# A chunked recurrence with its odd heads stored in the other order: paired products, state and output in one product, right-looking inverses

## The chip, the core and the metric

The kernel runs on one core of one Trainium2 chip. A core has a tensor engine (PE, with its weight loads shown apart as PEld), a vector engine (DVE), a scalar engine (ACT), GpSimd (POOL) and a sync engine (SP), which here issues nearly all DMAs. Each engine runs its instructions in order. The metric is device time in microseconds (us), lower is better.

## The reference

One gated block over S = 2048 tokens of width 1024. Its input projection feeds two branches: an RWKV-7 recurrence with 8 heads of 64 (the part that changes), and an attention over 256 selected keys per query. The recurrence is, for each head, with a 64x64 state:

```python
def rwkv7_scan(r, w, k, v, a_vec, b_vec):
    def step(state, inp):
        r_t, w_t, k_t, v_t, a_t, b_t = inp
        sa = jnp.einsum('bhvk,bhk->bhv', state, a_t)
        state = (state * w_t[:, :, None, :] + sa[..., None] * b_t[:, :, None, :]
                 + v_t[..., None] * k_t[:, :, None, :])
        y_t = jnp.einsum('bhvk,bhk->bhv', state, r_t)
        return state, y_t
...
    _, y = lax.scan(step, s0, xs)

def rwkv7_branch(...):
    ...
    y = rwkv7_scan(r_h, w_h, k_h, v_h, -kk, kk * a_h)
    yn = ((y - mu) * lax.rsqrt(var + GN_EPS)).reshape(B, S, RWKV_WIDTH) * lnx_g + lnx_b
```

The outputs of both branches are gated, projected, summed and normed.

## The kernel before

The tokens lie in 4 blocks `tb` of 512. The recurrence runs over 32 chunks of 64 tokens, 8 to a block, all in float32. Three functions do it.

`rwkv_pass(tb)` makes, for each pair of heads `p`, the decayed factors `ar` and `bk` and their products of 128x128 per head and chunk (L698, tile `pg`), masks them and stores them in DRAM (`gmd`), with `ard`, `bkd`, `vtd` beside them. The even head of a pair sits in rows 0 to 63 of the tensor engine (hh = 0), the odd one in rows 64 to 127 (hh = 1).

`rwkv_inv(tb)` loads the 128 triangular blocks of 32x32 of a token block, one to a partition (16 loads, L725), and inverts them by 31 steps of a multiplication (L733) and a sum (L735) on DVE, then stores them (`tid`, `ttd`, L738 to L740).

`rwkv_chain(tb)` is the recurrence proper. For each chunk it issues 7 loads, then, for all 8 heads: two steps that make the off-diagonal block of the inverse (L770 and L775, 32x32, tile `zu`), the state times the chunk's `ar` (L781, four products of 128x128, a pair of heads at a time, the state `H` held as blocks on a diagonal), `gmc` times v (L784), copied to `xx` (L787, ACT), the inverse times `xx` (L790), copied to `uv` (L791, DVE), the state update (L794, four products of 128x128 into `hp`, added to the decayed state by L798 on POOL and L799 on DVE), and the output (L801, into the same bank `pp` as L781 and L784, copied to `y` by L806). `H` is what one chunk hands to the next. Every second chunk is normed, every fourth goes through `chain_out` (transposes, L837). Its PSUM pool (`pc`) holds one bank each for `zu`, `pp` and `hp`.

Beside it run the projection GEMM (`gemm_half`, L251, three passes of 256 tokens), the keys and values of attention (`heads`, L868 and L878, tile `p`), and later the first branch's output projection (`branch_a`, L1092, tile `br`) and attention (from L925 on).

No order is written by hand: a scheduler puts the instructions of each engine in order by priority. `self.band(n)` sets the priority of what is emitted after it, a lower number first, and among equals what is emitted first:

```python
        self.band(50000)
        self.rwkv_chain(0)
        self.band(60000)
        self.cut = 2
        self.gemm_half((2, 3), ("rkv",))
        self.band(55000)
        self.rwkv_pass(2)
        self.rwkv_inv(2)
        self.band(55000)
        self.rwkv_chain(1)
        self.rwkv_pass(3)
        ...
        self.rwkv_inv(3)
        self.rwkv_chain(2)
        self.rwkv_chain(3)
        self.band(70000)
        self.gemm_half((2, 3), ("q",))
```

## Time and profile before

| what | value |
|---|---|
| time, median of 3 runs | 2611.75 us (2610.64 to 2611.93) |
| span of the profiled execution | 2605.7 us |
| PE busy | 2449.8 us, 94% of the span |
| DVE, ACT, POOL busy | 1750.5 (67%), 1229.8 (47%), 868.2 us (33%) |
| matmul instructions | 16776 |
| DMA packets, mean rate | 423499, 160 GB/s |

The span runs from the first to the last instruction; of the profiled execution only the span is recorded, and the median of the runs lies 6.05 us above it. Busy is the time in which an engine had an instruction in flight. Matmuls overlap in its pipeline, so in a full queue what a product costs is the distance from its start to the next one's start, and not its own length. A float32 product on PE runs as two passes and is shown as two instructions: eight products are an entry "x16".

### The profile page before, as it was taken

To read this page: it belongs to the slowest core of one execution; us is meant where nothing else is said; L and a number is where in the kernel's file an instruction comes from. 1 tells how busy PE (TensorE), PEld (TensorE's weight loads), DVE (VectorE), ACT (ScalarE), POOL (GpSimd) and SP (SyncE) were. 2 spreads that over 40 slices of the span, in tenths; PEclk is the share of its full clock that TensorE was granted. 3 is DMA by queue.
4 is the path that set the end of the run, shared out by engine and by line. 5 is a ranking of instruction groups with operands and counts; after the bars stand their busy time and mean duration, and the time that the engine had idled before them with its cause. 6 is when DMAs were issued, how large, how long until landed. Compare 5 with 4: busy or idle time off the path is not lost. (4 is left out here: it accounts for less than half of the span.)

```text
span 2605.7 us, 45357 instructions
## 1 busy us (share of the span) xinstructions
PE 2449.8 (94%) x16776; PEld 2153.8 (83%) x16776; DVE 1750.5 (67%) x3509; ACT 1229.8 (47%) x2136; POOL 868.2 (33%) x707
## 2 busy tenths in 40 slices
PE   4899999989899999899999999999989999999998
PEld 3687777868677899689898888988978999988887
DVE  6615888798988355774956947533468888877443
ACT  4315636446344423324334233343367888865332
POOL 2311131241323333223233322131155545645342
PEclk9999999999999999899999999999999999999999
DMA  7754222522233756568677669977763334145442
GB/s 245 271 149 127 77 85 73 131 77 88 84 103 102 243 162 202 147 192 234 179 219 204 187 189 284 293 233 189 239 199 116 91 88 118 45 152 195 147 150 77
DMA packets 423499, 415.69 MB, mean 160 GB/s; under 512 B 80010, under 2 KB 339890, under 8 KB 418404
## 3 DMA queue, kind: packets, MB, share of 16 engines
q1 hardware_dynamic: 422692, 404.33, 51.7%
q0 software_dynamic: 576, 8.39, 0.8%
q8 instruction: 132, 2.16, 0.4%
q14 instruction: 99, 0.81, 0.1%
HBM read 254.04 MB, written 160.15 MB: 159 GB/s over the span
## 5 line engine op out<-in xcount | busy, mean ns | idle before, releaser
L251 PE MATMUL g<-hh,whi 128*128 128x256 f32 (+1 forms) x2176 | 726.9, 334 | 14.8 <-DVE eo L265 4.5
L251 PE MATMUL g<-hl,whi 128*128 128x256 f32 (+1 forms) x2176 | 722.5, 332 | 3.9 <-POOL hl L169 2.4
L251 PE MATMUL g<-hh,wlo 128*128 128x256 f32 (+1 forms) x2176 | 721.0, 331 | 1.2 <-POOL wlo L237 1.2
L251 PEld LDWEIGHTS g<-hh,whi 128*128 128x128 f32 x2176 | 421.4, 194 | 63.8 <-issue 5.7
L251 PEld LDWEIGHTS g<-hl,whi 128*128 128x128 f32 x2176 | 421.0, 193 | 47.6 <-issue 3.9
L251 PEld LDWEIGHTS g<-hh,wlo 128*128 128x128 f32 x2176 | 420.7, 193 | 42.7 <-issue 3.9
L237 POOL TENSOR_TENSOR wlo<-wraw,whi 128x1024 fp32r<-128x1024 f32 (+1 forms) x89 | 216.9, 2437 | 629.4 <-ACT whi L236 583.0
L421 ACT ACTIVATE re<-ixs 128x512 f32<-128x512 f32 (+3 forms) x304 | 158.9, 548 | 176.1 <-DVE sc L427 109.8
L427 DVE SCALAR_TENSOR_TENSOR sc<-re,wi,sc 128x512 f32<-128x512 f32 (+3 forms) x266 | 222.6, 842 | 21.7 <-ACT re L421 6.5
L236 ACT CAST whi<-wraw 128x1024 fp32r<-128x1024 f32 (+1 forms) x89 | 92.8, 1042 | 175.1 <-PE g L251 131.0
L957 PE MATMUL pt<-ident,lt 128*128 128x128 f32 x1088 | 168.2, 276 | 6.4 <-ACT tp L963 3.5
L947 ACT ACTIVATE lt<-lt,nm 128x128 f32<-128x128 f32 (+15 forms) x128 | 154.7, 1211 | 14.2 <-DVE nm L946 14.1
L943 DVE CUSTOM_DVE_ANT_0 lt<-lg,mask 128x512 f32<-128x512 f32 (+3 forms) x256 | 147.4, 590 | 15.9 <-PE lg L941 7.5
L974 PE MATMUL yv<-ph,vp 128*128 128x256 f32 (+1 forms) x576 | 151.5, 285 | 6.7 <-ACT yl L978 4.7
L968 DVE TENSOR_TENSOR pl<-pt,ph 128x512 fp32r<-128x512 f32 (+1 forms) x216 | 139.1, 657 | 25.7 <-ACT ph L967 24.6
L974 PE MATMUL yv<-pl,vp 128*128 128x256 f32 x576 | 152.4, 300 | 2.0 <-POOL pl L965 2.0
L418 PE MATMUL ixs<-kim,st 128*128 128x512 f32 (+3 forms) x304 | 117.3, 387 | 28.7 <-ACT re L421 24.8
L940 PE MATMUL lg<-m,sq 128*128 128x256 f32 (+3 forms) x384 | 137.2, 366 | 5.0 <-DVE cm L943 4.1
L957 PEld LDWEIGHTS pt<-ident,lt 128*128 128x128 f32 x1088 | 125.9, 141 | 15.6 <-ACT tp L963 4.5
L941 PE MATMUL lg<-m,sq 128*128 128x256 f32 (+3 forms) x384 | 127.4, 337 | 0.0
L733 DVE TENSOR_TENSOR prd<-tm,ln 128x1 f32<-128x1 f32 (+30 forms) x124 | 113.3, 914 | 20.5 <-DMA pk<-pj 14.6
L967 ACT CAST ph<-pt 128x512 fp32r<-128x512 f32 (+1 forms) x216 | 115.9, 565 | 19.7 <-PE pt L957 13.7
(347 smaller groups left out, 5391.4 us busy)
## 6 DMA issues: line engine op xcount, KB each, us to landing
wraw<-in_w_in_dram SPq DMA_DIRECT2D x88, 512.0 KB
gg<-eo SPq DMA_DIRECT2D x64, 256.0 KB
gmd<-gt SPq DMA_DIRECT2D x64, 256.0 KB
gmc<-gmd SPq DMA_DIRECT2D x32, 512.0 KB
g<-gg SPq DMA_DIRECT2D x64, 256.0 KB
m<-ks SPq DMA_DIRECT2D x32, 512.0 KB
pj<-eo SPq DMA_DIRECT2D x52, 256.0 KB
x<-in_ada_w_dram SPq DMA_DIRECT2D x24, 512.0 KB
```

The lines of the kernel that those rows point to most:

```text
L237: nc.gpsimd.tensor_tensor(lo[:, :, :n], raw[:, :, :n], hi[:, :, :n].bitcast(FT), op=OP.subtract)
L251: T.matmul(p[:, s], a[:, k], b[:, k, s], start=n == 0, stop=n == 3 * KD - 1)
L418: T.matmul(p[:, :kn], st[:, h], M[0][:, k0:k0 + kn], start=True, stop=False)
L421: A.activation(r[:, :kn], p[:, :kn], AF.Relu)
L427: V.scalar_tensor_tensor(o, r[:, :kn], wi, o, op0=OP.mult, op1=OP.add)
L940: T.matmul(p[:, :kn], sq[:, qb * 128:(qb + 1) * 128], m1[:, k0:k1_], start=True, stop=False)
L941: T.matmul(p[:, :kn], sq[:, qb * 128:(qb + 1) * 128], m2[:, k0:k1_], start=False, stop=True)
L943: V.tensor_tensor_reduce(lt[:, k0:k1_], p[:, :kn], mk, 1.0, -3.0e38, OP.add, OP.max, cm[:, i:i + 1])
L947: ex = A.activation(lt[:, :n], lt[:, :n], AF.Exp, bias=nm, accum_out=lsum[:, qb, h:h + 1])
L957: T.transpose(p[:, o:o + 128], L[i][:, kt * 128:(kt + 1) * 128], self.ident)
L968: V.tensor_tensor(pl[:, :n], p[:, :n], ph[:, :n].bitcast(FT), op=OP.subtract)
L974: T.matmul(yv[:, qs], vp[:, kt, :], b[:, o:o + nn], start=kt == 0 and i == 0, stop=kt == last and i == 1, skip_group_check=True)
```

## The change

The odd heads get the other order of rows and columns: what lies in rows 0 to 63 for an even head lies in rows 64 to 127 for an odd one, and so do the halves of its output. A pair of products can then stand in different rows and different columns of the tensor engine. With it:

- `rwkv_pass` emits the products of both heads of a pair alternately, into two banks (L709).
- `rwkv_inv` is right-looking: step s takes column s from all later rows (L747 multiply, L749 add), (31-s)(s+1) elements a step.
- `rwkv_chain` is rewritten. `chunk_loads` fetches the next chunk's operands with 19 DMAs (7 before) into two buffers `cb0` and `cb1` made by hand, with `ttc0` and `ttc1`. `chunk_off` (L800, L807) and `chunk_v` (L820, L823) prepare the next chunk. Per chunk there follow the state times `ar` (L850: 8 products, each 64 rows and 128 columns of weights, 64 columns moving), the inverse (L857), and one product for state update and output together (L866: 8 products, 128 rows and 128 columns of weights, 64 columns moving). The state `H` is stored without the zero blocks. The copies are spread over ACT and DVE, and the output is added on DVE (L881).
- Norms and `chain_out` of a block wait in a list and are emitted a chunk later. The PSUM pool of the chain has 4 banks held for all time (`X0` to `X3`), and that of `heads` 2 instead of 3.
- Bands: the chains get 45000 and 47000 instead of 50000 and 55000, and chain 0 is emitted after the GEMM `rkv` of the second half.

```diff
@@ rwkv_pass
+                pts = [pg((128, 4, 128)) for hh in range(2)]
+                for j in range(4):
+                    for hh in range(2):
+                        r_ = slice(hh * 64, hh * 64 + 64)
+                        T.matmul(pts[hh][:, j], bk[r_, c0 + j, :], ar[r_, c0 + j, :], start=True, stop=True)
@@ rwkv_inv
-        for t in range(1, 32):
-            v = prd[:, :t * t].rearrange("p (j s) -> p j s", j=t)
-            V.tensor_tensor(v, tm[:, 0:t, 0:t].rearrange("p s j -> p j s"),
-                            ln[:, 0:t, t][:, None, :].to_broadcast([128, t, t]), op=OP.mult)
-            V.tensor_reduce(tm[:, t, 0:t], v, axis=AX, op=OP.add)
+        for s in range(31):
+            r, n = 31 - s, s + 1
+            v = prd[:, :r * n].rearrange("p (t j) -> p t j", t=r)
+            V.tensor_tensor(v, ln[:, s, n:][:, :, None].to_broadcast([128, r, n]),
+                            tm[:, s, 0:n][:, None, :].to_broadcast([128, r, n]), op=OP.mult)
+            V.tensor_tensor(tm[:, n:, 0:n], tm[:, n:, 0:n], v, op=OP.add)
@@ chunk_loads, chunk_off, chunk_v (new)
+        for a, b in ((E, O), (O, E)):
+            DMA.dma_start(cb[a, :, 2], src[b, :, 0, 0])
+            DMA.dma_start(cb[a, :, 1], src[b, :, 0, 1])
+        DMA.dma_start(cb[:, :, 4:6], src[:, :, 1])
...
+                T.matmul(zp[o + 32:o + 64, p], cb[64 - o:96 - o, p, 2 + 2 * e, 32:64], t1c[64 - o:96 - o, p],
+                         start=True, stop=True)
@@ rwkv_chain
+            if not last:
+                nxt = R["v"] = self.chunk_loads(tb + (c == 7), (c + 1) % 8)
...
             for p in range(4):
-                T.matmul(pp[:, p * 128:(p + 1) * 128], arc[:, p, :], H0[:, p, :], start=p == 0, stop=False,
-                         skip_group_check=True)
+                for e in range(2):
+                    r_ = halves[e]
+                    T.matmul(pp[e][:, p], arc[r_, p], H0[r_, p], start=False, stop=p == 3, skip_group_check=True)
...
+            up = X[2][:, 0:256].rearrange("q (p v) -> q p v", p=4)
             for p in range(4):
-                T.matmul(hp[:, p], bkc[:, p * 128:(p + 1) * 128], uv[:, p * 128:(p + 1) * 128], start=True, stop=True)
+                for e, r_ in enumerate(halves):
+                    T.matmul(up[halves[1 - e], p], ttc[r_, p], xx[r_, p], start=True, stop=True)
...
+            mg = X[2].rearrange("q (p e v) -> q p e v", p=4, e=2)
+            for e in range(2):
+                for p in range(4):
+                    T.matmul(mg[:, p, e], cb[:, p, 5 * e:5 * e + 2].rearrange("q g t -> q (g t)"), uv[:, p, e],
+                             start=True, stop=True)
...
+            if not last:
+                self.chunk_off(nxt)
+                self.chunk_v(nxt)
@@ the order
-        self.band(50000)
-        self.rwkv_chain(0)
...
-        self.band(55000)
+        self.band(45000)
+        self.rwkv_chain(0)
+        self.band(57000)
+        self.rwkv_pass(3)
+        self.rwkv_inv(3)
+        self.R["pctx"].close()
+        self.band(47000)
         self.rwkv_chain(1)
```

How the order moves, at three places. On PE before, the last product of the projections (L251) stands ahead of the state update of chunk 28 (L794); then the output of that chunk (L801) and `branch_a` (L1092):

```order
L790 MATMUL zu<-xx,ttc 64x64 x8
L251 MATMUL g<-hl,whi 128x256
L251 MATMUL g<-hh,wlo 128x256
L251 MATMUL g<-hh,whi 128x256
L251 MATMUL g<-hl,whi 128x256
L251 MATMUL g<-hh,wlo 128x256
L794 MATMUL hp<-uv,bkc 128x128 x4
L801 MATMUL pp<-uv,gmc 64x64 x8
L1092 MATMUL br<-uh_19482,w_pah 128x256
L1092 MATMUL br<-ul_19483,w_pah 128x256
L1092 MATMUL br<-uh_19482,w_pah 128x256
```

Here 28 of 32 chunks lie beside the projections. In the change the last L251 stands behind the merged product of chunk 24 (L866), and only the products of `heads` (L952, L962) are left beside chunks 25 to 32:

```order
L866 MATMUL X_9188<-uv,cb_9182 128x64 x8
L251 MATMUL g<-hl,whi 128x256
L251 MATMUL g<-hh,wlo 128x256
L251 MATMUL g<-hh,whi 128x256
L251 MATMUL g<-hl,whi 128x256
L251 MATMUL g<-hh,wlo 128x256
L850 MATMUL X_9186<-H_9174,arc 128x64 x4
L850 MATMUL X_9187<-H_9174,arc 128x64 x4
L952 MATMUL p<-lat_16844,w_ukh 128x512 x2
L952 MATMUL p<-lat_16846,w_ukh 128x512 x2
L952 MATMUL p<-lat_16844,w_ukl 128x512 x2
```

So four more chunks stand behind the end of the projections. The next place is the end of the chain on PE. Before, one of the last chunks stands like this, with products of `branch_a` (L1092) between its steps:

```order
L1092 MATMUL br<-ul_19767,w_pah 128x256
L1092 MATMUL br<-uh_19766,w_pal 128x256
L781 MATMUL pp<-H_9176,arc 128x128 x2
L775 MATMUL zu<-ttc,t1c 32x32 x8
L781 MATMUL pp<-H_9176,arc 128x128 x2
L784 MATMUL pp<-uv,gmc 64x64 x8
L1092 MATMUL br<-uh_19766,w_pah 128x256
L1092 MATMUL br<-ul_19767,w_pah 128x256
L1092 MATMUL br<-uh_19766,w_pal 128x256
L1092 MATMUL br<-uh_19766,w_pah 128x256
```

Other work fills PE between the steps. In the change the last two chunks and the start of `branch_a` (there L1176) read so:

```order
L857 MATMUL X_9188<-xx,ttc_9178 64x64 x8
L866 MATMUL X_9188<-uv,cb_9176 128x64 x8
L850 MATMUL X_9186<-H_9180,arc 128x64 x4
L850 MATMUL X_9187<-H_9180,arc 128x64 x4
L919 MATMUL X_9188<-ident,y 128x128 x4
L857 MATMUL X_9188<-xx,ttc_9184 64x64 x8
L866 MATMUL X_9188<-uv,cb_9182 128x64 x8
L1176 MATMUL br<-uh_19830,w_pah 128x256 x2
L1176 MATMUL br<-ul_19831,w_pah 128x256
```

No L1176 stands ahead of the last L866 any more, and a chunk's steps follow each other with nothing between them but transposes (L919). A little earlier two chunks mesh: L807 and the first half of L820 of one chunk stand ahead of the merged product of the chunk before it:

```order
L850 MATMUL X_9186<-H_9180,arc 128x64 x4
L850 MATMUL X_9187<-H_9180,arc 128x64 x4
L800 MATMUL X_9189<-t1c,cb_9176 32x32 x7
L857 MATMUL X_9188<-xx,ttc_9184 64x64
L820 MATMUL X_9186<-uv,cb_9176 128x64
L823 MATMUL X_9186<-uv,cb_9176 64x64 x3
L857 MATMUL X_9188<-xx,ttc_9184 64x64 x7
L807 MATMUL X_9189<-ttc_9178,z 32x32 x8
L820 MATMUL X_9187<-uv,cb_9176 128x64
L823 MATMUL X_9187<-uv,cb_9176 64x64 x3
L866 MATMUL X_9188<-uv,cb_9182 128x64 x8
```

The third place is the SP queue late in the chain, one chunk's loads. Before, 7 of them, with other transfers between:

```order
L1118 DMA gg_81<-g 128x2x256
L764 DMA ttc<-ttd_9205 32x8x32
L765 DMA ttc<-ttd_9205 32x8x32
L1095 DMA g<-gg_82 128x2x256
L1118 DMA gg_81<-g 128x2x256
L1095 DMA g<-gg_82 128x2x256
L757 DMA bkc<-bkd_9189 128x512
L755 DMA gmc<-gmd_9181 128x1024
L759 DMA uv<-vtd_9193 64x512
L1118 DMA gg_81<-g 128x2x256
L766 DMA t1c<-tid_9201 32x8x32
```

Between a chunk's loads stand those of `branch_a`. In the change 19 to a chunk; the buffer `cb` named here is read by the merged product two chunks back:

```order
L765 DMA cb_9182<-gmd_9193 64x4x64 x2
L766 DMA cb_9182<-gmd_9193 128x4x128
L769 DMA uv<-vtd_9205 64x4x64
L770 DMA uv<-vtd_9205 64x4x64
L787 DMA cb_9182<-bkd_9201 64x4x64
L788 DMA cb_9182<-bkd_9201 64x4x64
L789 DMA cb_9182<-bkd_9201 128x4x64
L773 DMA arc<-ard_9197 64x512
L774 DMA arc<-ard_9197 64x4x64
L775 DMA arc<-ard_9197 64x4x64
L785 DMA ttc_9178<-ttd_9217 32x4x32 x3
L765 DMA cb_9176<-gmd_9193 64x4x64 x2
```

Whatever stands behind a load that waits for its buffer waits too.

## Rows read from the trace of the kernel before

**Rows 1.** Windows: stretch, length, busy per engine, TensorE clock, DMA share, GB/s.
```profile
1165.60:1748.00 582.40, 576.31 (x5506) 525.93 (x5505) 366.11 (x568) 215.11 (x364) 181.97 (x170) 0.99 0.75 224
1748.00:1829.60 81.60, 72.75 (x703) 67.76 (x702) 32.14 (x51) 27.36 (x45) 16.41 (x16) 0.90 0.74 209
1829.60:1890.80 61.20, 59.25 (x492) 58.77 (x491) 26.44 (x44) 20.25 (x32) 7.76 (x6) 0.97 0.70 225
1890.80:2605.70 714.90, 681.46 (x4592) 619.71 (x4592) 500.79 (x1373) 470.17 (x863) 349.50 (x346) 0.98 0.41 125
```

**Rows 2.** Timeline, PE, 1773 us: start, length, what ran.
```profile
1773.51 1.05 PE L794 MATMUL hp<-uv,bkc 128*128 128x128 f32 x8
1774.49 1.15 PE L801 MATMUL pp<-uv,gmc 128*64 128x64 f32 x16
1775.57 0.69 PE L770 MATMUL zu<-t1c,gmc 32*32 32x32 f32 x16
1776.18 0.39 PE L1092 MATMUL br<-uh,w_pal 128*128 128x256 f32 x1
```

**Rows 3.** Timeline, PE, 1779 us, the same block of tokens.
```profile
1779.95 0.94 PE L781 MATMUL pp<-H,arc 128*128 128x128 f32 x6
1780.82 1.14 PE L784 MATMUL pp<-uv,gmc 64*64 64x64 f32 x16
1781.89 0.39 PE L1092 MATMUL br<-ul,w_pah 128*128 128x256 f32 x1
```

**Rows 4.** Timeline, PE, 1242 us, inside the projections.
```profile
1242.31 0.28 PE L251 MATMUL g<-hl,whi 128*128 128x256 f32 x1
1242.52 1.14 PE L790 MATMUL zu<-xx,ttc 64*64 64x64 f32 x16
1243.59 0.40 PE L631 MATMUL pg<-ei,oneh 128*8 128x512 f32 x1
```

**Rows 5.** Timeline, PE, 1274 and 1305 us: the products of rwkv_pass.
```profile
1273.87 1.71 PE L698 MATMUL pg<-ar,bk 64*128 64x128 f32 x16
1275.51 0.39 PE L251 MATMUL g<-hl,whi 128*128 128x256 f32 x1
...
1305.44 1.16 PE L698 MATMUL pg<-ar,bk 64*128 64x128 f32 x8
1306.52 0.39 PE L251 MATMUL g<-hh,wlo 128*128 128x256 f32 x1
```

**Rows 6.** Timeline, PE, 37 to 45 us: one column moving, then 128.
```profile
37.37 3.57 PE L138 MATMUL modp<-ones,acc 128*128 128x1 f32 x16 [3.66 <-DVE acc L208]
42.94 1.94 PE L165 MATMUL tp<-ident,x 128*128 128x128 f32 x8 [2.00 <-DVE h L167]
44.53 0.78 PE L251 MATMUL g<-hh,whi 128*128 128x512 f32 x1
```

**Rows 7.** Timeline, SP (issues of DMAs), 1791 us.
```profile
1791.40 0.42 SPq L757 DMA_DIRECT2D bkc<-bkd  x1
1791.91 0.38 SPq L755 DMA_DIRECT2D gmc<-gmd  x1
1792.34 0.45 SPq L759 DMA_DIRECT2D uv<-vtd  x1
```

**Rows 8.** Timeline, SP, 1580 us: the last loads of the fourth inverse.
```profile
1579.68 2.26 SPq L725 DMA_DIRECT2D ln<-gmd  x5
```

**Rows 9.** Timeline, DVE: first and last operation of the fourth inverse.
```profile
1584.98 0.16 DVE L733 TENSOR_TENSOR prd<-tm,ln 128x1 f32<-128x1 f32 x1 [2.47 <-DMA arc<-ard]
...
1650.05 1.03 DVE L737 COPY ln<-tm 128x1024 f32<-128x1024 f32 x1
```

**Rows 10.** Groups of instructions, DVE: count, busy, mean ns, idle before.
```profile
L733 DVE TENSOR_TENSOR prd<-tm,ln 128x1 f32<-128x1 f32 (+30 forms) x124 | 113.3, 914 | 20.5 <-DMA pk<-pj 14.6 <-DMA arc<-ard 2.5 <-DMA ln<-gmd 1.1
L735 DVE TENSOR_REDUCE tm<-prd 128x1 f32<-128x1 f32 (+30 forms) x124 | 61.6, 497 | 2.4
...
L799 DVE TENSOR_TENSOR H<-hp,hw 64x256 f32<-64x256 f32 x64 | 26.8, 419 | 23.8 <-PE hp L794 22.7
```

More of the change, by code (lines that the diff above doesn't have):

```diff
@@ L584, in rwkv_open @@
         G.memset(R["eps"], 64e-5)
-        R["H"] = []
+        R["H"], R["cb"], R["tt2"] = [], [], []
         for i in range(2):
-            h = c1.tile([128, 4, 128], FT, name=f"H{i}")
+            h = c1.tile([128, 4, 64], FT, name=f"H{i}")
             G.memset(h, 0.0)
             R["H"].append(h)
+            cb = c1.tile([128, 4, 7, 64], FT, name=f"cb{i}")
+            G.memset(cb[:, :, 3], 0.0)
+            R["cb"].append(cb)
+            t = c1.tile([128, 4, 64], FT, name=f"ttc{i}")
+            G.memset(t, 0.0)
+            R["tt2"].append(t)
+        R["X"] = [R["pc"].tile([128, 512], FT, name=f"X{i}") for i in range(4)]
         R["n"] = 0
@@ L693, in rwkv_pass @@
             for c0 in (0, 4):
+                pts = [pg((128, 4, 128)) for hh in range(2)]
[3 more added lines that the diff above has]
+                        T.matmul(pts[hh][:, j], bk[r_, c0 + j, :], ar[r_, c0 + j, :], start=True, stop=True)
                 for hh in range(2):
[L695 to L698 removed]
                     gt = st.tile([128, 4, 128], FT, name="gt", bufs=4)
[L700 removed]
+                    V.tensor_tensor(gt, pts[hh], gm4, op=OP.mult)
                     DMA.dma_start(R["gm"][tb][c0:c0 + 4, :, 2 * p + hh, :].rearrange("c q t -> q c t"), gt)
@@ new lines, in chunk_off @@
+    def chunk_off(self, ops):
+        T, A, R = self.nc.tensor, self.nc.scalar, self.R
+        cb, uv, arc, ttc, t1c = ops
+        zp = R["X"][3][:, 0:128].rearrange("q (p t) -> q p t", p=4)
+        for p in range(4):
+            for e in range(2):
+                o = e * 64
+                T.matmul(zp[o + 32:o + 64, p], cb[64 - o:96 - o, p, 2 + 2 * e, 32:64], t1c[64 - o:96 - o, p],
+                         start=True, stop=True)
+        z = R["ch"].tile([128, 4, 32], FT, name="z", bufs=1)
+        for o in (32, 96):
+            A.copy(z[o:o + 32], zp[o:o + 32])
+        for p in range(4):
+            for o in (0, 64):
+                T.matmul(zp[o:o + 32, p], z[o + 32:o + 64, p], ttc[o + 32:o + 64, p, 32:64], start=True, stop=True)
+        for o in (0, 64):
+            A.copy(ttc[o:o + 32, :, 32:64], zp[o:o + 32])
@@ new lines, in chunk_v @@
+    def chunk_v(self, ops):
+        T, X = self.nc.tensor, self.R["X"]
+        cb, uv = ops[:2]
+        halves = (slice(0, 64), slice(64, 128))
+        for p in range(4):
+            for e, r_ in enumerate(halves):
+                o = X[e][:, p * 64:p * 64 + 64]
+                if p == 0:
+                    T.matmul(o, cb[r_, p, 2 + e:4 + e].rearrange("q g t -> q (g t)"), uv[r_, p, e],
+                             start=True, stop=False, skip_group_check=True)
+                else:
+                    T.matmul(o[r_], cb[r_, p, 2 + 2 * e], uv[r_, p, e], start=False, stop=False, skip_group_check=True)
@@ L829, in chain_out, with out @@
         t_ = slice(half * 256, half * 256 + 256)
-        for p in (0, 2):
+        def out(p):
             bo = ch.tile([128, 2, 256], FT, name="bo")
             DMA.dma_start(bo, self.rows(R["bo"][tb], p, t_))
-            pt = pc.tile([128, 2, 256], FT, name="pp" if p else "zu")
+            pt = R["X"][2].rearrange("p (k t) -> p k t", k=2)
             for k in range(2):
@@ L840, in chain_out @@
             DMA.dma_start(self.rows(self.YA[tb], p, t_), bo)
+        R["late"] += [lambda: out(0), lambda: out(2)]
     def heads(self, ctx):
@@ L847, in heads @@
         w = self.pool("kvw", 3, side="right", ctx=ctx)
-        ps = self.pool("kvp", 3, PSUM, ctx=ctx)
+        ps = self.pool("kvp", 2, PSUM, ctx=ctx)
         U = []
```

144 lines of the change are left out of this document (78 added, 66 removed).

## The prediction

> **What bounds the kernel now.** I first read the busy time of PE by stretches, with borders at steps of the program: the first chunk's state update (L794) ends at 1165.6 us, the last L251 at 1748.0, the last chunk's output begins at 1829.6, and the last product of `branch_a` (L1092) ends at 1890.8 [rows 1]. From chunk 1 to the end of the projections PE is busy 576.3 of 582.4 us. The 27 further chunks there, the passes, the projections and `heads` are one queue of products with no gap worth naming: what counts is how long the products take, not what a chunk waits for. In the next 81.6 us, chunks 29 to 32 run between products of `branch_a`; PE still has 72.8 us of work, at a granted clock of 0.90. Attention after 1890.8 is the same in both kernels and starts when `branch_a` is through. So the change is worth what it does to the 725.2 us from 1165.6 to 1890.8. Before 1165.6 the projections have come equally far in both orders when chunk 1 updates its state, so I count nothing there. My sum goes by the profiled execution (span 2605.7 us); the median of the runs is 6.05 us more, and I add the difference to the median.
>
> **The price of a pass.** In a full queue the distance from start to start is the price. Four L794 (8 passes, 128 columns of weights, 128 moving) take 0.98 us and eight L801 (16 passes, 64 by 64 columns) 1.08; eight L770 (32 by 32) take 0.61 [rows 2]; six passes of L781 0.87 and eight L784 1.07 [rows 3]. These hold a change of the array's tiling. L251 goes every 0.12, but the step from it to L790 is 0.21, so 0.09 are lost at the change, and the first weight load behind it is not hidden [rows 4]; I take 0.14 us for each change. That leaves 0.112 us for a pass with 128 columns of weights and as many moving, 0.058 for 64 and 64, 0.031 for 32 and 32.
>
> A merged product (L866) has 128 columns of weights but only 64 moving. Which of the two sets the pace? At the start of the kernel sixteen products with 128 columns of weights and one moving column take 3.57 us, 0.22 each, and eight with 128 moving take 1.59 to the next start, 0.20 each [rows 6]. One moving column costs as much as 128: the weights set it. So a pass of L866 costs 0.112, and eight products 1.79 us. L794 and L801, which it replaces, cost 0.90 + 0.93 = 1.83. The merging saves nothing on PE.
>
> Do pairs in different rows overlap? Eight products of L698, four in each row half, take 1.64 us, where four alone take 1.08, changes of tiling included [rows 5]. In series it would be 16 x 0.112 + 0.14 = 1.93. So some overlap exists, though there they stand four and four. I take full overlap for pairs that alternate, and none as the other bound.
>
> **The change, part by part.**
> *Products of a chunk.* Before: 0.50 + 0.50 (L770, L775) + 0.90 (L781) + 3 x 0.93 (L784, L790, L801) + 0.90 (L794) = 5.59 us. After, paired: 0.40 + 0.40 (L800, L807) + 0.57 (L820, L823) + 0.90 (L850: 16 passes at half of 0.112) + 0.47 (L857) + 1.79 (L866) = 4.53. Unpaired: 6.65. The gain is 1.06 us a chunk, 33 us over 31; without overlap it is a loss as large.
> *Changes of tiling.* Between the same two points the order has 537 before and 671 after, since the shorter steps are spread between products of the projections: 134 x 0.14 = 19 us lost.
> *Products of `rwkv_pass`.* In most places the order still has four of one head and then four of the other; 21 adjacent groups of 87 against 8 of 68. 13 more at about 0.4 us: 5 us gained.
> So PE's work falls by 33 - 19 + 5 = 19 us. The same prices give 697 us for the work of before; the other 28 of the 725 are its idle 16.9 us (the lengths less the busy times of the first three stretches) and stretches at a lower clock [rows 1]. After: 678.
> *Inverses.* They cost DVE 113.3 + 61.6 = 174.9 us in all, 43.7 per block [rows 10]. Right-looking, 62 operations over half as many elements make some 20 to 30. That lies beside a full PE and is worth nothing until PE waits for an inverse. With pass 3 at 57000 that happens once: from the last product of pass 3 to chunk 25 stand 52 us of PE work. Loads landing, inverse and stores took from about 1582 to 1654 before, of which 1585.0 to 1651.1 on DVE, shared with other work [rows 8, 9]; 14 less for the shorter inverse and a few for less sharing leave some 62. Wait: 10 us.
> *Where the chunks stand.* The decisive part. Before, the projections end behind chunk 28 and `branch_a` fills the gaps of the last four. After, they end behind chunk 24; beside chunks 25 to 32 there are only some 24 products of `heads` after chunk 25's, and no product of `branch_a`. The last seven steps are bare, at 48 us of PE work, and a chunk's own loop sets their pace.
> *That loop.* The merged product of chunk c-1 frees `cb`. Then SP issues six loads for chunk c+1, 0.47 to 0.5 us each [rows 7]: 3.0. Landing: the five loads of an inverse are issued by 1581.94 and DVE starts at 1584.98 after a wait for a DMA, so 3.0 to 3.5 from the last one's start [rows 8, 9]: 3.3. Then L800, a copy (0.42, as L799's mean for 64x256 [rows 10]), L807, L820 and the rest of L857: 3.0 with changes of tiling. Then L866 of chunk c, which stands behind all that in PE's queue: 1.9. Sum 11.6; with a clock as in the second stretch of [rows 1] for the PE part some 12.3 us a chunk. Bounds: 9 (loads early, only H, xx, uv and their copies in the loop) to 14 (all 19 issues ahead, 9 us). Seven steps at 12.3 are 86, 38 more than their PE work.
> *DMAs.* 12 more issues a chunk, 384 in all. SP needs 10.5 to 12 us a chunk for 22 to 25 issues; chunks among the projections come every 13 to 20 us, so there they are covered, and in the tail they are in the loop above. The copies and sums on DVE and ACT lie beside PE in the dense part.
>
> **Sum.** 725.2 - 19 (PE work) - 28 (idle and low clock of before) + 10 (idle of the same kind in the dense part) + 10 (inverse) + 38 (tail) + 7 (start of `branch_a`, whose weights are split behind the last chunk) = 743. That is 18 us more: 2611.75 + 18 = **2630 us**.
>
> **Rivals.**
> *Tail short, faster (other side).* If the loads for chunk c+1 are in place when its L800 comes, the loop is L850, copies, L857, copies, L866 and the sum into H: 1.8 + 0.5 + 0.5 + 0.5 + 1.9 + 0.4 and the switches, with the transposes 8 to 9 us. Break-even is 12.3 - 18 / 7 = 9.7 us a chunk. At 9, and without the wait for the inverse, it is 743 - 23 - 10 = 710: 15 us faster, 2597. For it: the buffers of `cb` are two, and a DMA lands in 3 us. Against it: L807 of the next chunk stands ahead of L866, and its loads behind the L866 of the chunk before.
> *It cancels.* A tail of 9.5 to 10.2 us a chunk: 2608 to 2616.
> *Pairs overlap less, slower still.* In L857, L800 and L807 both halves of a pair write one bank (X2, X3); the trace shows overlap only for two different banks [rows 5]. If such pairs run in series, it is 0.75 us a chunk, 18 over the 24 dense chunks: 2648. With no overlap at all, 51 us: 2681, if [rows 5] owes its 0.29 us to something else. SP running out among the projections gives a like amount, 20 to 40.
>
> The Trainium skill (TensorEngine Tiling (Array Packing), section "Gotcha 1: PSUM Pressure") says that different row tiles cannot access the same PSUM bank at the same time. By that, L857, L800 and L807 run in series: the rival of 2648. No row of before has two row halves in one bank, so the trace neither bears it out nor denies it. The same page (section "Key Properties") says that a change of tiling mode drains the engine, and the 0.09 us of [rows 4] agrees.
>
> **How the numbers follow.** Slower by the bare tail: 0.50, 2617 to 2645. Faster: 0.22, 2592 to 2604. Cancels: 0.13. Less overlap or SP: 0.15, 2640 to 2681. The range 2592 to 2660 leaves out the worst of the last case and the best of the second. 0.2% of this time is 5 us, about what a measurement can tell from no change. Faster 0.22, same 0.13, slower 0.65.
>
> **What would show it.** L866 at 1.8 us for its eight products; L850 near 1.0 where it alternates. PE busy near 99% from chunk 1 to chunk 24, then, behind the last L251, a stretch of some 90 us with PE at 60% or less, chunks 11 to 13 us apart, L800 waiting for DMAs. No L1176 until the last L866. A wait of some 10 us ahead of chunk 25. The end of `branch_a` near 1909 us instead of 1890.8. Wrong if the chunks of the tail are 9 us apart or less, if the weights of L866 do not set its pace (then 0.9 us a chunk, 28 in all, come off), or if other work reaches PE in the tail.

## The result, and the profile after

The changed kernel takes 2744.52 us (median; 2740.33 to 2748.6) against 2611.19 for the kernel before in the same comparison: a ratio of 1.0512, 95% interval 1.0489 to 1.0536. That is 133 us slower, where 18 were predicted with a range of 2592 to 2660. The sign was right, the size far off.

Windows of the changed kernel, same columns as [rows 1] (length; busy time of PE, PEld, DVE, ACT and POOL; granted clock of TensorE, where 1.00 is 2.4 GHz and 0.50 is 1.2 GHz; share of the DMA engines; GB/s): from the start of chunk 1's merged product (its state update) to the last L251, to chunk 25's state update, to chunk 32's, to the end of `branch_a`, and attention:

```profile
1150.00:1725.90 575.90, 553.75 (x5009) 498.15 (x5008) 284.41 (x513) 190.97 (x385) 139.24 (x108) 0.93 0.66 174
1725.90:1786.00 60.10, 39.79 (x188) 24.69 (x186) 41.40 (x100) 19.55 (x39) 0.62 (x1) 0.70 0.83 250
1786.00:1898.70 112.70, 92.35 (x680) 79.09 (x681) 38.69 (x78) 33.16 (x80) 7.92 (x9) 0.55 0.64 180
1898.70:2038.30 139.60, 106.06 (x777) 102.80 (x777) 50.12 (x77) 38.35 (x62) 21.77 (x16) 0.85 0.78 235
2038.30:2746.70 708.40, 679.54 (x4595) 615.48 (x4594) 492.49 (x1373) 465.13 (x859) 346.35 (x346) 0.98 0.39 120
```

Read such rows in three parts. Busy time times granted clock is the work at full clock (an estimate: the mean clock is that of the whole stretch). Length less busy time is idle. What is left is lost to the half clock. Before, the 725.2 us of [rows 1] are 693 of work, 17 idle and 15 lost to the clock. After, the 888.3 us from 1150.0 to 2038.3 are 684 of work, 96 idle and 108 lost to the clock. So the work did not grow. Idle time grew by 79 us and the loss to the clock by 93; work fell by about 10; the stretch begins 15.6 us sooner (1.9 of them because it is counted from the start of chunk 1's product, before from its end) and attention is 6.5 shorter than in [rows 1]. 79 + 93 - 10 - 15.6 - 6.5 = 140, the difference of the spans (2746.7 and 2605.7) to 1 us.

Waits of PE, first from 1150 to 1725, then from 1725 to 2040 (us in total, times, longest):

```profile
PE X L800 <- DMA cb<-gmd: 14.7, 8, 4.1
...
PE br L1176 <- DVE g L1181: 25.1, 9, 10.1
...
PE br L1176 <- ACT uh L1115: 8.3, 2, 6.5
PE X L800 <- DMA cb<-gmd: 7.0, 6, 3.0
```

L800 waits for loads of `cb` among the projections, where the prediction had them covered. The price of one such wait is more than its length. The timeline of PE and the windows around the wait at 1159:

```profile
1159.72 0.60 PE L800 MATMUL X<-t1c,cb 32*32 32x32 f32 x14 [2.66 <-DMA cb<-gmd]
...
1161.56 0.41 PE L251 MATMUL g<-hl,whi 128*128 128x256 f32 x1
1161.78 0.41 PE L251 MATMUL g<-hh,wlo 128*128 128x256 f32 x1
```

```profile
1156.00:1159.30 3.30, 1.06 (x11) 0.68 (x7) 0.43 (x1) 1.58 (x4) 0.00 (x0) 0.97 0.88 171
1159.80:1172.80 13.00, 13.00 (x99) 10.98 (x100) 7.71 (x9) 5.56 (x11) 3.35 (x2) 0.50 0.31 78
1173.50:1180.00 6.50, 6.50 (x63) 6.08 (x62) 4.74 (x11) 1.74 (x3) 1.87 (x2) 1.00 0.79 195
```

PE stood for 2.66 us; then it was busy 13.00 of 13.00 us at a granted clock of 0.50, L251 every 0.21 us instead of 0.12. At half the clock that is about 6.5 us of work, so 2.66 us of wait cost about 6.5 more. Over the stretch from chunk 1 to the last L251, 22 us of idle go with some 39 lost to the clock.

The issues on SP that these loads wait for, where [rows 7] had 0.43 to 0.51 from start to start:

```profile
1155.13 0.56 SPq L766 DMA_DIRECT2D cb<-gmd  x1
1155.79 0.58 SPq L769 DMA_DIRECT2D uv<-vtd  x1
1156.42 0.60 SPq L770 DMA_DIRECT2D uv<-vtd  x1
1157.07 0.59 SPq L785 DMA_DIRECT2D ttc<-ttd  x1
```

0.63 to 0.66 us each. Summed over SP's records from chunk 1 to the last L251, issues fill 0.68 of the stretch (721 of them), before 0.46 (558); the 0.70 in the expectations below counts pauses between issues of one line too. Inside a block of eight chunks it is more: from chunk 1 to 8, 9 to 16 and 17 to 24 the state updates come 18 to 19 us apart with 24 to 27 issues each, and SP issues for 0.72, 0.76 and 0.80 of the time (before 0.41, 0.40 and 0.55). Between the blocks, the first state update of the next comes 99, 84 and 62 us behind the last one (before 33, 45 and 35).

The products themselves were as predicted. PE's timeline, the same kernel: a merged product among the projections and L850 with alternating halves, then L866 in the tail, where the granted clock was 0.50:

```profile
1150.16 1.90 PE L866 MATMUL X<-uv,cb 128*128 128x64 f32 x16
1151.99 0.24 PE L800 MATMUL X<-t1c,cb 32*32 32x32 f32 x2
...
1155.13 1.12 PE L850 MATMUL X<-H,arc 64*128 64x64 f32 x16
1156.17 0.55 PE L724 MATMUL pg<-ident,pv 128*128 128x128 f32 x3
...
1785.88 3.67 PE L866 MATMUL X<-uv,cb 128*128 128x64 f32 x16
1789.48 0.31 PE L800 MATMUL X<-t1c,cb 32*32 32x32 f32 x2
```

1.83 us from L866 to the next start (predicted 1.8), 1.04 for L850 (predicted 1.0), 3.60 in the tail. The inverse, as groups on DVE; [rows 10] has the two groups of before:

```profile
L749 DVE TENSOR_TENSOR tm<-tm,prd 128x31 f32<-128x31 f32 (+15 forms) x124 | 57.5, 463 | 3.1
L747 DVE TENSOR_TENSOR prd<-ln,tm 128x31 f32<-128x31 f32 (+15 forms) x124 | 53.9, 435 | 35.5 <-DMA pv<-pj 10.8 <-DMA pk<-pj 8.6 <-DMA lat<-lat 6.9
```

111.4 us against 174.9, 27.9 a block (predicted 20 to 30).

Where the steps stand, in us of each kernel's profile to about 1 us (pass: its last product, L709 after the change; c24, c25, c32: state update of that chunk), with the kernels that are compared below:

| kernel | pass 2 | pass 3 | last L251 | c24 ends | c25 starts | c32 ends | heads | branch_a |
|---|---|---|---|---|---|---|---|---|
| before | 1393 | 1568 | 1748 | 1667 | 1701 | 1830 | 1595–1675 | 1752–1891 |
| after | 1495 | 1689 | 1726 | 1726 | 1786 | 1899 | 1733–1838 | 1899–2039 |
| before_19_loads | 1446 | 1646 | 1695 | 1707 | 1735 | 1844 | 1695–1856 | 1883–2007 |
| no_loads | 1394 | 1570 | 1755 | 1542 | 1558 | 1675 | 1591–1671 | 1759–1895 |
| passes_first_chain_early | 1372 | 1547 | 1830 | 1675 | 1689 | 1820 | 1566–1674 | 1834–1967 |
| two_queues | 1485 | 1679 | 1694 | 1694 | 1768 | 1911 | 1715–1792 | 1825–1982 |
| passes_first_two_queues | 1379 | 1544 | 1772 | 1652 | 1666 | 1781 | 1572–1680 | 1776–1909 |
| two_queues_ride_six | 1381 | 1549 | 1740 | 1657 | 1672 | 1838 | 1578–1686 | 1752–1911 |

Passes 2 and 3 end 102 and 121 us later after the change. The projections, which fill PE beside the chunks, run out before chunk 25, and `heads` and `branch_a` stand behind the passes and the chunks.

### The profile page after: what moved, and what is told of

Its sections match the earlier page's. It is cut to its first block, busy times and chain, and to the rows that moved or that the text cites. A ratio compares the mean times of both kernels' runs of the same rounds, so it can differ in the third digit from the quotient of the medians.

```text
span 2746.7 us, 45918 instructions
## 1 busy us (share of the span) xinstructions
PE 2524.6 (92%) x16776; PEld 2198.1 (80%) x16776; DVE 1710.6 (62%) x3605; ACT 1240.7 (45%) x2256; POOL 825.6 (30%) x647
## 4 chain that ended last, share of the span: by engine, by line
PE 50%; DMA 9%; DVE 5%; SPq 2%; issue 2%; ACT 2%; POOL 1%; POOLq 0%; ACTq 0%; DVEq 0%
PE g L251 16%; PE fo L1261 5%; PE yv L1058 4%; PE pt L1041 4%; PE br L1176 3%; PE pg L709 2%; PE lg L1024 2%; PE lg L1025 2%; PE X L866 2%; DMA cb<-gmd 2%; DMA g<-gg 1%; PE X L857 1%; PE X L823 1%; PE X L850 1%; PE X L820 1%
## 5 line engine op out<-in xcount | busy, mean ns | idle before, releaser
L251 PE MATMUL g<-hh,whi 128*128 128x256 f32 (+1 forms) x2176 | 731.8, 337 | 17.4 <-DVE prev L339 7.0
L251 PE MATMUL g<-hl,whi 128*128 128x256 f32 (+1 forms) x2176 | 727.9, 335 | 4.0 <-DMA hl<-hls 2.1
L251 PE MATMUL g<-hh,wlo 128*128 128x256 f32 (+1 forms) x2176 | 726.1, 334 | 0.3 <-POOL wlo L237 0.3
L251 PEld LDWEIGHTS g<-hh,whi 128*128 128x128 f32 x2176 | 426.2, 196 | 66.2 <-issue 6.8
L251 PEld LDWEIGHTS g<-hl,whi 128*128 128x128 f32 x2176 | 426.0, 196 | 47.6 <-issue 5.6
L251 PEld LDWEIGHTS g<-hh,wlo 128*128 128x128 f32 x2176 | 425.8, 196 | 40.8 <-issue 3.8
L418 PE MATMUL ixs<-kim,st 128*128 128x512 f32 (+3 forms) x304 | 117.5, 388 | 28.3 <-ACT re L421 24.3
L419 PE MATMUL ixs<-kim,st 128*128 128x512 f32 (+3 forms) x304 | 115.2, 381 | 0.0
```

Of the source, the lines that this page charges most:

```text
L251: T.matmul(p[:, s], a[:, k], b[:, k, s], start=n == 0, stop=n == 3 * KD - 1)
```

## The experiments

**One part at a time.** inv_alone is the kernel before with only the new inverse (L747 and L749 for L733 and L735). old_bands is the changed kernel with the old priorities and the old order of emission (chain 0 ahead of the GEMM, chain 1 ahead of pass 3; shown cut):

```
-        self.band(45000)          # rwkv_chain(0)
+        self.band(50000)
-        self.band(57000)          # rwkv_pass(3)
+        self.band(55000)
-        self.band(47000)          # rwkv_chain(1..3)
+        self.band(55000)
...
```

> The kernel before with the right-looking inverses alone. Every theory: the inverses' time on DVE falls from 174.9 us to about 111 us as in the changed kernel, and since they lie beside a full PE the whole run moves by 0 to -8 us (2604 to 2612). If the inverse were on the path, more than 10 us would come off.

> The changed kernel with the bands and the order of emission of before. Theory 3 (the bands put pass 3 behind the chains, so that pass 3, its inverse, heads and branch_a come late): pass 3 ends earlier, the wait ahead of chunk 25 goes, and 60 to 90 us come off (2655 to 2685). Theories 1 (loads wait for the buffer that the merged product frees) and 2 (19 loads a chunk hold the SP queue): 10 to 30 us come off at most, and the waits for cb and the low clock among the projections stay.

inv_alone: 2612.48 (1.0009, 0.998 to 1.0038), no change; the inverses were hidden, as predicted. old_bands: 2727.37 (1.0454, 1.0404 to 1.0504), 17 less than the changed kernel, where 60 to 90 were expected if its priorities were to blame. The new inverse costs nothing, and the old order gives little back.

**The loads.** early_loads issues the loads that L800 and L820 need ahead of the others (the load of L766 cut in two, three buffers of `uv`). no_loads takes all but the first two chunks' loads away; each later chunk works on those operands again, so its output is not the reference's (shown cut):

```
+        if len(R['ops']) > 1:
+            return R['ops'][c % 2]
...
```

> The changed kernel with the operands that the next chunk needs first (the first halves of gm, v, the inverse) loaded into places that the merged product does not hold: one load more per chunk, a third buffer for uv. Theory 1: L800 no longer waits for cb among the projections, the clock there returns from 0.93 to 0.98 or more, and 50 to 90 us come off (2655 to 2695). Theory 2: 20 loads a chunk are left, the passes stay as late or later, and the time falls by less than 20 us or rises.

> The changed kernel with the loads of the first two chunks only: all later chunks compute with the same two sets of operands, so the recurrence's output is not the reference's; 570 DMAs are left out. Theories 1 and 2: passes, heads and branch_a come early again, no wait for cb, clock 0.98, PE's work from chunk 1 to the end of branch_a 678 us as summed, whole run 2560 to 2600. Theory 3: the loads matter little, the bare tail stays and the run is above 2680.

early_loads: 2796.79 (1.0711, 1.0664 to 1.0758), 52 us more than the changed kernel: theory 1 fails, theory 2 had allowed a rise. In its order the projections are done at 1625 and pass 3 at 1736, and from 1625 to 1943 the granted clock was 0.53 to 0.59. no_loads: 2615.08 (1.0019, 0.9988 to 1.005), 129 us less than the changed kernel, which is all that the change lost, though not the 2560 to 2600 expected. The edit takes away more than the loads: later chunks no longer depend on the passes and inverses either, and chunk 25 runs ahead of the end of pass 3 (1558 and 1570). The two kernels on two queues below keep that dependence. The windows of no_loads, chunk 1 to 24, to 32, to the last L251, to the end of `branch_a`:

```profile
1154.00:1542.00 388.00, 383.40 (x3979) 335.11 (x3979) 265.99 (x499) 165.69 (x356) 111.97 (x93) 1.00 0.49 144
1542.00:1675.00 133.00, 132.39 (x1271) 116.68 (x1270) 92.86 (x191) 55.34 (x120) 23.36 (x17) 1.00 0.76 228
1675.00:1755.00 80.00, 78.43 (x650) 77.82 (x649) 20.61 (x25) 24.53 (x39) 19.64 (x11) 1.00 0.56 176
1755.00:1895.00 140.00, 108.33 (x767) 104.12 (x768) 37.71 (x55) 31.82 (x51) 17.54 (x12) 0.83 0.71 213
```

Is it the number of loads, or what the new products do with them? before_19_loads is the kernel before, its own products and order of bands, with its seven loads a chunk cut into nineteen (halves of rows, even and odd heads apart), the same bytes:

```
-            DMA.dma_start(arc, R["ar"][tb][c])
...
+            DMA.dma_start(arc[E], src[E])
+            DMA.dma_start(arc[O, :, 0:64], src[O, :, 0:64])
+            DMA.dma_start(arc[O, :, 64:128], src[O, :, 64:128])
...
```

> The kernel before with its 7 loads per chunk cut into 19 pieces of the shapes that the changed kernel loads; same bytes, same buffers, nothing else changed. Theory 2 (the number of loads on the SP queue, at the chains' high priority, makes the passes late): pass 2 and pass 3 end some 100 us later as in the changed kernel, branch_a starts after 1850 us, whole run 2680 to 2750. Theory 1 (loads wait for the buffer of the merged product) and every theory that blames the new products: below 2630.

> The kernel before with the chain's loads of the first two chunks only (its output is not the reference's, 210 DMAs are left out). Every theory: before hardly waits for its loads, so 2598 to 2612. Against no_loads (2615) it tells what the new products are worth where loads cost nothing: by the sum of the prediction the changed kernel has 19 us less work on PE; if it still isn't faster, the four chunks that before runs inside branch_a outweigh them.

before_19_loads: 2732.08 (1.0468, 1.0449 to 1.0488), 121 us more than before without one new product. Passes 2 and 3 end 53 and 78 us later than before, where some 100 were expected. before_no_loads (no_loads' edit in the kernel before): 2611.86 (1.0011, 0.9994 to 1.0028): seven loads cost nothing. Windows of before_19_loads (chunk 1 to the last L251, to `branch_a`, to its end) and its longest wait:

```profile
1173.00:1695.00 522.00, 513.32 (x4867) 468.84 (x4866) 311.36 (x495) 175.24 (x291) 161.18 (x150) 0.99 0.68 185
1695.00:1884.00 189.00, 130.62 (x970) 107.79 (x968) 72.02 (x115) 46.34 (x87) 16.43 (x26) 0.64 0.67 193
1884.00:2008.00 124.00, 102.18 (x768) 98.71 (x766) 44.12 (x64) 35.48 (x59) 21.50 (x16) 0.90 0.68 220
```

```profile
PE br L1112 <- DMA xt<-in_w_pa_dram: 26.6, 1, 26.6
```

Here the dense part is as full as before (513 of 522 us, clock 0.99), with nineteen loads. The time goes behind it: 189 us at 0.64 with the projections used up. In the order of PE's instructions, pass 3 ends at projection product 5756 of 6528 before, at 6317 here and at 6376 in the changed kernel: the loads alone move the passes back.

**The products, without loads.** Two changes to no_loads: no_loads_no_pairs issues one head parity after the other (`for e … for p` for `for p … for e` in L800, L807, L820 to L823, L850 and L857); no_loads_split cuts L866 into state and output, 16 products of 64 columns of weights for 8 of 128.

> no_loads (2615 us; output not the reference's) with the products of the two heads of a pair no longer alternating: four of one, then four of the other, in L800, L807, L820, L823, L850 and L857. If pairs in different rows overlap: eight products of L857 take 1.07 instead of 0.6 us and eight of L850 1.9 instead of 1.0, up to 2 us a chunk, 2650 to 2680. If the hardware doesn't overlap them, or not in one bank: within 10 us of no_loads.

> no_loads (2615 us; output not the reference's) with the merged product cut in two, state and output, each eight products with 64 columns of weights. If the 128 columns of weights set the pace of the merged product (as the prediction has it): the two halves take 2 x 0.93 against 1.79 us, and the time stays within 10 us of no_loads. If the moving columns set it: 0.9 us more a chunk, 2635 to 2650.

no_loads_no_pairs: 2696.58 (1.0322, 1.0283 to 1.0362), 82 us above no_loads, more than the 35 to 65 expected: pairs overlap. Only some 30 of it are work: from chunk 1 to the last L251, PE was busy 695.7 us at a granted clock of 0.90, some 626 at full clock, against 594.2 at 1.00 in no_loads. The rest is the clock. no_loads_split: 2623.16 (1.0043, 1.0027 to 1.006), 8 us above: the merging saves next to nothing. PE's timeline of no_loads, then of no_loads_no_pairs (in both, L853 is L850, L860 is L857, L869 is L866: three lines further down), then of no_loads_split (L870 is the divided L866):

```profile
1173.14 1.11 PE L853 MATMUL X<-H,arc 64*128 64x64 f32 x16
1174.19 0.31 PE L810 MATMUL X<-ttc,z 32*32 32x32 f32 x6
...
1177.56 0.68 PE L860 MATMUL X<-xx,ttc 64*64 64x64 f32 x16
1178.18 0.44 PE L823 MATMUL X<-uv,cb 64*128 64x64 f32 x4
...
1181.39 1.89 PE L869 MATMUL X<-uv,cb 128*128 128x64 f32 x16
1183.21 0.44 PE L810 MATMUL X<-ttc,z 32*32 32x32 f32 x16
```

```profile
1174.49 1.60 PE L853 MATMUL X<-H,arc 64*128 64x64 f32 x16
1176.03 0.37 PE L810 MATMUL X<-ttc,z 32*32 32x32 f32 x6
...
1178.40 0.68 PE L860 MATMUL X<-xx,ttc 64*64 64x64 f32 x8
1179.00 0.43 PE L823 MATMUL X<-uv,cb 64*128 64x64 f32 x2
```

```profile
1172.93 1.90 PE L870 MATMUL X<-uv,cb 128*64 128x64 f32 x32
1174.76 0.43 PE L803 MATMUL X<-t1c,cb 32*32 32x32 f32 x14
```

These are passes, two to a product. Sixteen alternating L860 take 0.62 us, as long as eight of one parity (0.60). Sixteen L853 take 1.05 us where they alternate and 1.54 in two groups of eight. Sixteen passes of 128 columns of weights take 1.82 us, thirty-two of 64 columns 1.83, with 64 columns moving in both: here the columns of weights set the pace, not the number of products.

**Where the passes stand.** If late passes are the loss, moving them forward must give it back with all nineteen loads in place. passes_first and passes_first_chain_early differ in one number:

```
-        self.band(55000)          # rwkv_pass(2)
+        self.band(45000)
-        self.band(45000)          # rwkv_chain(0)
+        self.band(61000)
-        self.band(57000)          # rwkv_pass(3)
+        self.band(46000)
-        self.band(47000)          # rwkv_chain(1..3)
+        self.band(71000)          # passes_first_chain_early: 69000
```

passes_first_early_loads and passes_first_both add early_loads' edit to the first and the second.

> The changed kernel, its 19 loads left, with four bands changed: pass 2 and 3 at 45000 and 46000, chain 0 at 61000, chains 1 to 3 at 71000. Theory 2 with the priority as its lever: the passes end by about 1570 us, branch_a starts near 1760, eight or nine chunks run inside it, 2590 to 2630. Theory 1: the loads still wait for the merged product, so the waits and the low clock stay and the run is above 2650.

> As passes_first, but chains 1 to 3 at 69000, ahead of the projections q, z and g: all chunks are done before the projections end, and branch_a runs alone. If branch_a takes 135 us whatever runs beside it (139, 140 and 136 us in the three traces so far, with 92 us of products), this is 15 to 30 us slower than passes_first; if branch_a is as long as its products, the two are within 5 us.

> passes_first with the early loads (first halves of gm, v and the inverse into places that the merged product doesn't hold, 20 loads a chunk). Theory 1, now in an order that isn't upset: fewer waits of L800 for DMAs and a higher clock, 10 to 30 us less than passes_first. Theory 2: within 10 us of it, since the number of loads is what counts.

> passes_first_chain_early (2684 us) with the early loads: pass 2 and 3 at 45000 and 46000, chain 0 at 61000, chains 1 to 3 at 69000, and the operands that the next chunk needs first in places that the merged product doesn't hold. Theory 1 (loads that wait for the merged product cost waits and clock, once the order is right): the waits of L800 go, the clock of the stretch from chunk 1 to branch_a rises from 0.93 to 0.97 or more, 2615 to 2645. Theory 2 (the number of loads alone): 2670 to 2700.

passes_first: 2871.46 (1.1035, 1.0977 to 1.1093), passes_first_early_loads: 2857.97 (1.0945, 1.0924 to 1.0966): both much worse, which no expectation allowed for. With 71000 the chunks land among the last projections and alternate with them one by one; the tiling (rows and columns of weights) changes 1197 times from one PE record to the next between chunk 1 and the end of `branch_a`, 543 times in the changed kernel. PE's timeline of passes_first, and one window:

```profile
1501.68 0.58 PE L251 MATMUL g<-hl,whi 128*128 128x256 f32 x1
1502.19 0.47 PE L823 MATMUL X<-uv,cb 64*64 64x64 f32 x2
1502.59 0.58 PE L251 MATMUL g<-hh,wlo 128*128 128x256 f32 x1
```

```profile
1432.00:1700.00 268.00, 268.00 (x1492) 212.65 (x1490) 111.38 (x227) 59.18 (x120) 40.01 (x33) 0.76 0.52 145
```

passes_first_chain_early: 2684.11 (1.0288, 1.0247 to 1.033), 60 us less than the changed kernel by order alone, and 187 less than passes_first, where it was expected level or slower. passes_first_both: 2683.19 (1.0277, 1.026 to 1.0294): the order of the loads on the queue adds nothing. So the 69 us by which passes_first_chain_early lies above no_loads were still open.

**The queue.** two_queues moves eight of the nineteen loads (`arc`, `bk`, `vt`) to ScalarE's queue; the same in the order of passes_first_chain_early is passes_first_two_queues; passes_first_pool_queue has that order too and puts these eight on GpSimd's queue.

```
-        DMA.dma_start(arc[E], src[E])
+        nc.scalar.dma_start(arc[E], src[E])
...
```

> The changed kernel with eight of a chunk's nineteen loads (the three of arc, the three of bk, the two of vt) issued from ScalarE's queue, eleven left on SyncE's; bands and order as in the changed kernel. Theory A (SyncE's queue is full at 0.70 of the stretch and whatever stands on it, also the stores of passes 2 and 3, starts late): passes 2 and 3 end 40 us or more earlier than in the changed kernel (1495 and 1689 there), and the time comes to 2665 to 2700. Theory B (the number of small transfers as such, whoever issues them): 2735 to 2750, passes where they were. Against both: ScalarE holds its own work behind the issues, then its copies are late and the time is above 2750.

> The bands of passes_first_chain_early (2684.11) with the same eight loads on ScalarE's queue. Theory A: the waits for loads go, PE idles under 12 us between chunk 1 and the end of the GEMM, and the time comes to 2620 to 2655, near 2615, where the kernel without loads was. Theory B: 2675 to 2695, idle time and clock as they were.

> As passes_first_two_queues with the eight loads on GpSimd's queue. Theory A: 2620 to 2665. Theory B: 2675 to 2695. If GpSimd issues late behind its own work on passes 2 and 3, worse than with ScalarE's queue by 10 us or more.

two_queues: 2689.7 (1.0327, 1.0263 to 1.039), 55 us less than the changed kernel with the same order. passes_first_two_queues: 2618.82 (1.0038, 1.0018 to 1.0058), 65 less than with one queue, and level with no_loads. passes_first_pool_queue: 2669.43 (1.023, 1.0187 to 1.0274), 15 less, in the range of neither theory. The same transfers cost almost nothing when ScalarE issues eight of nineteen, so it is not their number but the one queue that costs. GpSimd shows that a second issuer alone is not enough. Its waits from 1154 to 1820 (us in total, times, longest):

```profile
POOL cb L787 <- PE X L866: 90.3, 20, 15.0
...
POOL arc L773 <- PE X L850: 39.4, 14, 8.0
```

A load that waits for its buffer holds GpSimd's own work behind it, and part of the passes is done there: passes 2 and 3 end 42 and 62 us later than with ScalarE's queue. Half of theory A's expectation of two_queues failed: pass 3 ends at 1679, 10 us sooner and not 40, since the order places it. The gain came elsewhere: the dense part ran at 0.97, and the loads of `branch_a`'s weights, issued on SP from 1884.3 in the changed kernel, came from 1799.5, and it began at 1825 instead of 1899. Windows of passes_first_two_queues, chunk 1 to 24, to 32, to the end of `branch_a`:

```profile
1158.20:1651.50 493.30, 491.48 (x4575) 433.23 (x4574) 312.14 (x599) 190.55 (x394) 125.57 (x102) 0.98 0.82 218
1651.50:1780.50 129.00, 127.52 (x1297) 116.43 (x1297) 54.10 (x99) 54.73 (x117) 26.60 (x19) 0.97 0.84 224
1780.50:1908.60 128.10, 104.99 (x767) 101.72 (x766) 44.81 (x69) 32.56 (x52) 15.22 (x11) 0.87 0.76 234
```

PE's waits for loads are down to 1.1 us up to 1790. What stays bare is `branch_a`: 128 us, 105 busy, at 0.87.

**The last chunks inside `branch_a`,** where [rows 1] has them before the change. two_queues_ride_four and two_queues_ride_six give the last four or six chunks a later priority; all_on_act_ride_four has all nineteen loads on ScalarE's queue.

```
+            if tb == NTB - 1 and c == 4:      # ride_six: c == 2
+                self.band(74000)
```

> passes_first_two_queues (2618.82) with the last four chunks given a later priority, so that the projections end before them and they run inside branch_a, as the last four of the kernel before do. branch_a lasts 124 to 140 us in every trace for 92 us of products, so PE has some 40 us free in it; the 28 chunks ahead end with the projections some 35 us earlier. If the place of the last chunks is what was left (theory: loop without waits, tail covered): 2580 to 2600, faster than the kernel before. If branch_a is stretched by what the chunks take there (its DMA share is at 1.0 in parts), 2610 to 2625, no gain.

> The same with six chunks inside branch_a in place of four. Two more chunks ahead are 15 to 20 us of products that move into branch_a: if room is left there (chunks of 11 us apart, six take 66 of 130 us), 2565 to 2590; if the room is used up with four, 2590 to 2610.

> All nineteen loads on ScalarE's queue, and the last four chunks inside branch_a. If the queue's order behind other issues was all that mattered, the loads are out of the way of SyncE's: equal to two_queues_ride_four within 10 us. If nineteen issues in a row on an engine that also makes the copies of the off-diagonal blocks delay these, 15 us or more above it.

two_queues_ride_four: 2627.32 (1.0068, 1.0042 to 1.0095); two_queues_ride_six: 2611.5 (1.0013, 0.9996 to 1.0029); all_on_act_ride_four: 2624.26 (1.0049, 1.0026 to 1.0071). None reaches the gain that was expected if there was room in `branch_a`. With six chunks it begins at 1752 and ends at 1911, where it ended without this edit (1909): what the earlier start gave was paid back. The third is level with the first: in this order, all nineteen loads in one queue do little harm while the transfers of the passes stand in another. Two windows of two_queues_ride_six (`branch_a` with chunks, then alone) and the wait in them:

```profile
1740.20:1837.80 97.60, 92.26 (x867) 84.85 (x866) 40.67 (x76) 34.45 (x74) 16.50 (x13) 0.83 0.74 199
1837.80:1910.80 73.00, 59.45 (x453) 57.35 (x451) 26.97 (x45) 19.35 (x31) 7.66 (x6) 0.91 0.77 250
```

```profile
PE br L1178 <- DVE g L1183: 11.8, 4, 8.4
```

The best of these versions equals the kernel before; none beats it.

## Why the prediction was wrong, step by step

**The step that failed** is "chunks among the projections come every 13 to 20 us, so there they are covered": that loads which fit into the distance of chunks cost nothing. The sum behind it was near. Inside a block the chunks came 18 to 19 us apart with 24 to 27 issues, and SP was busy with these for 13 to 15 us (forecast: 22 to 25 issues, 10.5 to 12 us; one issue takes 0.64 and not 0.5 from start to start). They fit, and yet they cost some 120 to 130 us. SP also carries, in order, the loads and stores of the passes, the inverses and the weights. At a share of 0.72 to 0.80 (before 0.40 to 0.55) L800 waited 14.7 us for `cb`, and passes 2 and 3 ended 102 and 121 us later, so that each block of chunks began late. Shown by no_loads (129 us back), before_19_loads (121 us lost without the rest of the change) and passes_first_two_queues (65 us back with the same transfers on two queues). The rival "SP running out among the projections" named the mechanism, at 20 to 40 us and within a case of 0.15: at least three times too small, and with no working given. The sign came out right, but most of the loss comes from a term that the sum had at nothing.

**What it missed behind that step** is two other ways in which late loads cost. One is order: the loads shift passes 2 and 3 back, so the projections end sooner with respect to the chunks, and `heads` and `branch_a` come later. passes_first_chain_early prices it at 60 us. The other is the clock, which fell behind waits like the one at 1159: 108 us lost to it over the whole stretch against 15 before, 42 of them in the bare tail.

**Terms that were mis-sized.** Idle and loss to the clock taken together, by the windows above: *idle of the same kind in the dense part* 61 us where 10 were put; *the wait for the inverse* (the stretch before chunk 25) 32 where 10 were; *the tail* 62 where 38 were; *start of `branch_a`* 49 where 7 were. That is 139 more; PE's work was 684 and not 678. What the sum put at nothing came out on the other side: 15.6 us ahead of chunk 1 and 6.5 in attention.

*That loop*, 12.3 us a chunk, measured 16.1 (112.7 us for seven steps): the clock was 0.55 and not the 0.90 taken over from [rows 1], while PE waited only 7.0 us for `cb` there. *The wait for the inverse* grew by SP too. From the last product of pass 3 (1688.8) to the first step of its inverse 39 us went by, where it had been 17 (1568.2 to 1585.0 in [rows 9]), since SP issues its loads from 1703.8 to 1721.5 (before from 1569.4 to 1582). The changed kernel's first step:

```profile
1728.05 0.19 DVE L747 TENSOR_TENSOR prd<-ln,tm 128x31 f32<-128x31 f32 x1 [6.90 <-DMA lat<-lat]
```

*`branch_a`* takes 140 us alone, and 124 to 140 in every kernel that was run with it bare, for 768 matmul instructions of 0.12 us, 92 us. The prediction let it go at the pace of its products; it has a bound of its own (L1176 waits 25.1 us for `g` and 8.3 for `uh`), and before it hid four chunks. From 1950 to 1990 the profile has the DMA engines at a share of 1.03 to 1.04 and PE busy for 26 of 40 us; whether that is the cause was not tested.

**Right.** The price of a pass, the merged product at 1.8 us with nothing saved (no_loads_split), full overlap of alternating pairs (no_loads_no_pairs), hidden inverses (inv_alone) and, read off the order, projections ending behind chunk 24 and no L1176 before the last L866. The rival by which pairs that write one bank run in series is refuted: 0.62 us for sixteen L860 passes where the series was put at 0.93. The Trainium skill (TensorEngine Tiling (Array Packing), "Gotcha 1: PSUM Pressure") says that different row tiles cannot use one PSUM bank at the same time. For these pairs, which differ in columns of the array too, the measurement decides against it.

Two sums of the rivals do not come out of the prediction's own prices, without bearing on the result: the short tail has L850 at 1.8 us, not 0.90, and the series in one bank 0.75 us a chunk, not 0.66.

**Open.** Whether it is SP's issuing or the queue behind it that was too full, the runs do not separate: a second issuer was always a second queue. Whether the 19 us of PE work that the prediction took off are there: busy time times clock gives 684 after, 693 before, but 684 too for before_19_loads with the old products, so the estimate is not finer than about 10. With no loads at all the two kernels take 2615.08 and 2611.86, so nothing of it reaches the end; bare `branch_a` (140 us against 61.2 behind the last chunk in [rows 1]) is where the argument puts it, and moving chunks there gave back at most 7 us, which is within the scatter of the runs. Loads fewer by another layout of `gm`, `ar` and `bk` in DRAM weren't tried.

## What to carry to other kernels

Count what an in-order DMA queue carries in the whole stretch, not what a step adds to it: cutting seven loads into nineteen of the same bytes cost 4.7% in the kernel before, and a second issuing engine, with an order that has the passes first, took the changed kernel from 5.1% to 0.4%. That the issues of a step fit into the step does not make them free; and an engine that issues loads should not have work of its own that cannot stand behind a wait. Price a wait of TensorE by the clock behind it as well as by its length. When a program's order is made by a scheduler, look up where every later stage lands in the new order before pricing the part that was edited.

## What was not expected of the hardware

The granted clock stayed down long after a short wait: 2.66 us of idle, then 13 us of products at 0.50 with PE busy throughout. It also fell with PE never idle: in passes_first, 268 us with PE busy 268.00 at a mean of 0.76, where single products of the projections alternate with pairs of narrow ones; in no_loads_no_pairs 0.90 over 696 us, 695.7 of them busy, where no_loads, with pairs, had 1.00. What in these products brings it down the runs don't tell. Pairs in different rows and columns of the array overlapped fully even with one bank for both results: 0.62 us for eight pairs of passes, 0.60 for eight single ones.
